# The weights of the post norm multiplied in ahead of the squares, in a float32 decoder trunk

## The chip, the cores and the metric

The kernel runs on one core of a Trainium2 chip. Its engines are named as in the profile: PE (TensorE, the matmuls), PEld (its weight loads), DVE (VectorE), ACT (ScalarE), POOL (GpSimd) and SP (SyncE, which issues DMAs here). The metric is the device time of one execution in microseconds (us), the median over runs.

## The reference, cut to what matters

Two layers, each of three stages: a feed-forward (SwiGLU, width 2816), a mixer (four branches, gated and summed, then an output projection), and a second feed-forward. Each stage is wrapped in two RMS norms, one ahead of it and one behind it (the post norm), and added to the residual stream h, which is 512 tokens x 1024 channels of float32.

```
def rms_norm(x, g):
    y = xf * lax.rsqrt(jnp.mean(xf * xf, axis=-1, keepdims=True) + EPS)
    return (y * g.astype(jnp.float32)).astype(x.dtype)
...
f = swiglu(rms_norm(h, ffn1_pre_g[l]), ffn1_w_gate[l], ffn1_w_up[l], ffn1_w_down[l])
h = h + FFN_RESIDUAL_SCALE * rms_norm(f, ffn1_post_g[l])
u = rms_norm(h, mix_pre_g[l])
...
h = h + rms_norm(merged @ w_o[l], mix_post_g[l])
f = swiglu(rms_norm(h, ffn2_pre_g[l]), ffn2_w_gate[l], ffn2_w_up[l], ffn2_w_down[l])
h = h + FFN_RESIDUAL_SCALE * rms_norm(f, ffn2_post_g[l])
```

The post norm needs, for each token, the sum of the squares of the projection's row (for the factor 1/sqrt) and the row itself times the weights g. The two don't depend on each other.

## The kernel before, in words

Every float32 matmul is done as three matmuls of rounded parts: a value is split into a high part (hi, written by ACT) and the rest (lo, written by DVE). Weights come in chunks of 128 x 1024 (`raw`, issued by SP or POOL); ACT casts a chunk to `wh` (L122, L109), DVE subtracts to get `wl` (L123, L110). There are five buffers for each of the two, so a cast waits until PE has done with an older chunk.

The function `boundary` (from L257) is the end of one stage and the start of the next; it is called seven times, the first time without an end, the last time without a start. The last projection of a stage (down projection or output projection) is done by tokens: four token tiles t of 128 tokens, two column halves c of 512. A tile and half is one PSUM bank, `py`, 128 x 512. The first half runs over k with four banks open at once, and `gained(t, 0, ...)` follows for the four tiles (L372). The second half is done so that the tiles end one after another: behind each tile come `gained(t, 1, ...)`, `update(t)` and `normed(t)` (L387 to L390), while PE works on the next tile.

In these:
- `gained` reads the bank twice: `squares` on ACT (L255, an activation `sq` that adds up its outputs in a column of `stat`, with a short read of the accumulator behind it) and a multiplication by the weights `gb` on DVE (L351), which writes `yg`.
- `update` makes the factor from the two sums of squares: `nv` (L249) and `nw` (L250) on DVE, a power `nr` on POOL (L251); then DVE adds to the residual, two instructions `h` (L356).
- `normed` takes the squares of the new `h` on ACT, stores `h` by DMA from ACT's queue (L274), makes the next factor in the same way and writes `u` on DVE (L278), the pre-normed tile.

`turned` transposes two token tiles of `u` on PE (L290, banks `pt`) and splits the result into `xh` (ACT, L175) and `xl` (DVE, L168), both of which read `pt`. `outer` starts the next stage's first four products in banks `pf`: for each of eight k and four f, matmuls L152 (`xh`, `wh`), L153 (`xl`, `wh`), L154 (`xh`, `wl`), first on the token half of tiles 0 and 1. When tile 3 has been updated too, its and tile 2's `u` are transposed and the second token half follows.

Within an engine instructions run in order. Around the change that order isn't written by hand: a scheduler places the instructions of all engines, by priority of program order and its own model of when operands are ready. From the start of the next stage's body on (`manual_schedule`) the side engines keep program order. Where two engines touch one bank, reads included, the framework makes the second in program order wait for the first by a semaphore.

Of the kernel before, what the change touches and what calls it, by code (L numbers as in the profile page):

```python
# [63 lines left out]
def build(tc, ws, x, vecs, gains, wdf, lamv, fb, consts, out):  # L64
# [3 lines left out]
    with ExitStack() as ctx:  # L68
# [12 lines left out]
        def nm(s):  # L81
            cnt[0] += 1
            return f"{s}{cnt[0]}"

        def slot(dt=F32, s="s"):
            return sp.tile([P, T], dt, tag="s", name=nm(s))

        def ps(s="p"):
            return pp.tile([P, T], F32, tag="p", name=nm(s))
# [10 lines left out]
        for l in range(DEPTH):  # L100
            for n in range(2):
                c = (2 * FFN_CHUNKS + MIX_CHUNKS) * l + (FFN_CHUNKS + MIX_CHUNKS) * n + PLAIN
# [10 lines left out]
        def load(c, parts=1):  # L113

            raw = rawp.tile([P, CB * P], F32, tag="raw", name=nm("raw"))
            wh = wp.tile([P, CB * P], F32R, tag="wh", name=nm("wh"))
            wl = wp.tile([P, CB * P], F32R, tag="wl", name=nm("wl"))
            n = CB * P // parts
            for i in range(parts):
                j = slice(i * n, (i + 1) * n)  # L120
                nc.sync.dma_start(out=raw[:, j], in_=ws[c, :, j])
                S.copy(out=wh[:, j], in_=raw[:, j])  # L122
                V.tensor_sub(out=wl[:, j], in0=raw[:, j], in1=wh[:, j].bitcast(F32))  # L123
            ready[c] = wh, wl
# [16 lines left out]
        def settle():  # L141
            while late:
                late.pop(0)()

        def cover():
            settle()
            for _ in range(min(pace[0], len(spare))):
                spare.pop(0)()
# [82 lines left out]
        def tile4(name, l, k, c):  # L231

            for j in range(4):
                block((name, l, k, c + P * j))
            b0 = (len(order) - 4) % CB * P
            return cur[0][:, b0:b0 + T], cur[1][:, b0:b0 + T]

        def by_tokens(out, x, t, w, first, last):

            r = slice(t * P, (t + 1) * P)  # L240
            PE.matmul(out=out, lhsT=x[0][:, r], rhs=w[0], start=first, stop=False)  # L241
            PE.matmul(out=out, lhsT=x[0][:, r], rhs=w[1], start=False, stop=False)  # L242
            PE.matmul(out=out, lhsT=x[1][:, r], rhs=w[0], start=False, stop=last)  # L243

        def rstd_of(parts, factor=1.0):

            f2 = factor * factor
            v, var, r = (np_.tile([P, 1], F32, tag=n, name=nm(n)) for n in ("nv", "nw", "nr"))
            V.tensor_scalar(out=v, in0=parts[0], scalar1=1.0 / (D * f2), scalar2=EPS / f2, op0=ALU.mult, op1=ALU.add)  # L249
            V.scalar_tensor_tensor(out=var, in0=parts[1], scalar=1.0 / (D * f2), in1=v, op0=ALU.mult, op1=ALU.add)  # L250
            G.tensor_tensor(out=r, in0=var, in1=mhalf[:, 0:1], op=ALU.pow)  # L251
            return r

        def squares(src, col):
            S.activation(out=slot(F32, "sq"), in_=src, func=AF.Square, accum_out=col)  # L255

        def boundary(post, pre, first):  # L257
# [9 lines left out]
            stat = np_.tile([P, 16], F32, tag="stat", name=nm("stat"))  # L267

            def normed(t):

                for c in range(2):
                    squares(hs[t][c], stat[:, 8 + 2 * t + c:9 + 2 * t + c])
                    if post is not None:
                        nc.scalar.dma_start(out=hd[t][c], in_=hs[t][c])  # L274
                r = rstd_of([stat[:, 8 + 2 * t + c:9 + 2 * t + c] for c in range(2)])
                us = [slot(F32, "u") for _ in range(2)]
                for c in range(2):
                    V.tensor_scalar(out=us[c], in0=hs[t][c], scalar1=r, scalar2=None, op0=ALU.mult)  # L278
                return us
# [41 lines left out]
            if post is None:  # L321
                for t in range(4):
                    for c in range(2):
                        hs[t][c] = slot(F32, "h")
                        nc.sync.dma_start(out=hs[t][c], in_=x[t * P:(t + 1) * P, c * T:(c + 1) * T])
                    load(t, 2 if t == 0 else 1)
                us = [normed(t) for t in range(4)]
            else:
                row, factor, name, l, ys = post
                n = len(ys)  # L330
                gb = []

                def fetch():
                    for c in range(2):
                        gb.append(slot(F32, "gb"))
                        nc.scalar.dma_start(out=gb[c], in_=gains[row:row + 1, c * T:(c + 1) * T].broadcast_to([P, T]))
                        for t in range(NQ):
                            hs[t][c] = slot(F32, "h")
                            nc.scalar.dma_start(out=hs[t][c], in_=hd[t][c] if row else
                                                x[t * P:(t + 1) * P, c * T:(c + 1) * T])  # L340

                def part(k):
                    if k < n and not isinstance(ys[k], tuple):
                        ys[k] = halves(ys[k])

                yg = [[None, None] for _ in range(4)]

                def gained(t, c, p):
                    squares(p, stat[:, 2 * t + c:2 * t + c + 1])
                    yg[t][c] = slot(F32, "yg")  # L350
                    V.tensor_mul(out=yg[t][c], in0=p, in1=gb[c])  # L351

                def update(t):
                    r = rstd_of([stat[:, 2 * t + c:2 * t + c + 1] for c in range(2)], factor)
                    for c in range(2):
                        V.scalar_tensor_tensor(out=hs[t][c], in0=yg[t][c], scalar=r, in1=hs[t][c],  # L356
                                               op0=ALU.mult, op1=ALU.add)
                        if pre is None:
                            (nc.sync, nc.scalar)[c].dma_start(out=out[t * P:(t + 1) * P, c * T:(c + 1) * T],
                                                              in_=hs[t][c])  # L360

                settle()
                py = [ps("py") for _ in range(4)]
                for k in range(n):
                    if k == n // 2:
                        fetch()
                    part(k + AHEAD)
                    w = tile4(name, l, k, 0)
                    for t in range(4):
                        by_tokens(py[t], ys[k], t, w, k == 0, k == n - 1)  # L370
                    cover()
                for t in range(4):  # L372
                    gained(t, 0, py[t])
                py = [ps("py") for _ in range(4)]
                for k in range(n - HOLD):
                    w = tile4(name, l, k, T)
                    for t in range(4):
                        by_tokens(py[t], ys[k], t, w, k == 0, False)
                held = []
                for t in range(4):  # L380
                    for k in range(n - HOLD, n):
                        if t == 0:
                            held.append(tile4(name, l, k, T))
                        if t == NQ - 1 and k == n - HOLD // 2 and pre is not None:
                            turned(us[0:2], 0)
                        by_tokens(py[t], ys[k], t, held[k - n + HOLD], k == 0, k == n - 1)
                    gained(t, 1, py[t])  # L387
                    update(t)
                    if pre is not None:
                        us.append(normed(t))  # L390
                if pre is None:
                    return None
# [77 lines left out]
        def halves(src):  # L470
            hi, lo = slot(F32R, "gh"), slot(F32R, "gl")
            hi_of(hi, src)
            lo_of(lo, src, hi)
            return hi, lo
# [536 lines left out]
        for l in range(DEPTH):  # L1011
            c = l * VL + _VOFF["b_conv_w"]
# [3 lines left out]
        for l in range(DEPTH):  # L1016
            post = ffn(l, 1, boundary(post, ("ffn1_pre_g", l), ffn_first(l, 1)))
            post = mixer(l, boundary(post, ("mix_pre_g", l), mix_first(l)))
            post = ffn(l, 2, boundary(post, ("ffn2_pre_g", l), ffn_first(l, 2)))
# [51 lines left out]
```

## Time and profile before

| | |
|---|---|
| median of 3 runs | 2692.07 us (2691.65 to 2693.31) |
| the profiled execution's own time | 2689.96 us |
| its span, first to last instruction | 2688.2 us |
| busy: PE, DVE, ACT, POOL | 98%, 61%, 44%, 9% |
| instructions | 39670 |
| mean granted TensorE clock | 0.999 |

The span is what the trace covers; the execution's own time is 1.8 us longer. Matmuls overlap in the array, so a PE that is busy isn't at its peak; its pace is read from the distance between starts. "Granted clock" is the share of full TensorE speed that the throttle allowed in a stretch. In a timeline a bracket at the end of a row gives the idle time ahead of it and what ended that.

### The profile page before, as it was taken

The numbers are of one execution on the slowest core, as the hardware profiler recorded it, in microseconds if no ns is written. First come the engines' busy times: TensorE is split into PE (matmuls) and PEld (weight loads), VectorE is DVE, ScalarE is ACT, GpSimd is POOL, SyncE is SP. The second block draws the span as 40 slices with busy tenths as digits, with TensorE's granted clock in tenths as the row PEclk, the third lists the DMA queues.
The fourth block names the chain that finished last, engine by engine and source line by source line (L and its number), as shares of the span: only waits on it lengthen the run. The fifth ranks groups of instructions, "written<-read, shape, count | busy, mean of one in ns | idle before, by whom it ended". The sixth has DMA issues, their size and how long they took to land.

```text
span 2688.2 us, 39670 instructions
## 1 busy us (share of the span) xinstructions
PE 2646.6 (98%) x15764; PEld 2352.2 (88%) x15764; DVE 1651.0 (61%) x2715; ACT 1195.6 (44%) x2031; POOL 234.7 (9%) x306
## 2 busy tenths in 40 slices
PE   6999999999999999999999999999999999999998
PEld 6999888888888889998899998888888888899987
DVE  5656358777776456555375563596786854565552
ACT  5445242355454335544255452424545533455541
POOL 2110000000000002110021100000000000111100
PEclk9999999999999999999999999999999999999999
DMA  6987433222223256885358872332223223488850
GB/s 182 214 212 202 134 113 102 87 79 79 91 83 94 95 163 153 210 205 187 102 139 210 210 217 94 121 101 79 71 87 96 86 92 96 150 186 211 201 171 32
DMA packets 110105, 365.26 MB, mean 136 GB/s; under 512 B 12496, under 2 KB 12880, under 8 KB 109920
## 3 DMA queue, kind: packets, MB, share of 16 engines
q1 hardware_dynamic: 68688, 246.45, 27.5%
q0 software_dynamic: 23040, 83.90, 17.8%
q10 hardware_dynamic: 18192, 32.40, 3.6%
q8 instruction: 123, 2.02, 0.3%
q14 instruction: 62, 0.51, 0.1%
HBM read 350.07 MB, written 12.62 MB: 135 GB/s over the span
## 4 chain that ended last, share of the span: by engine, by line
PE 83%; DVE 5%; issue 5%; DMA 4%; ACT 2%; POOL 1%; POOLq 0%; ACTq 0%; DVEq 0%
PE p L152 11%; PE p L154 10%; PE p L153 10%; PE f L154 7%; PE f L152 7%; PE f L153 7%; PE py L241 6%; PE py L243 6%; PE py L242 6%; DMA raw<-ws 4%; PE o L782 1%; PE pv L242 1%; PE pv L241 1%; PE pv L243 1%; PE pt L766 1%
## 5 line engine op out<-in xcount | busy, mean ns | idle before, releaser
L122 ACT CAST wh<-raw 128x1024 fp32r<-128x1024 f32 (+1 forms) x305 | 319.1, 1049 | 719.0 <-PE p L153 348.0
L123 DVE TENSOR_TENSOR wl<-raw,wh 128x1024 fp32r<-128x1024 f32 (+1 forms) x305 | 371.4, 1219 | 383.2 <-ACT wh L122 377.6
L110 DVE TENSOR_TENSOR wl<-raw,wh 128x1024 fp32r<-128x1024 f32 x280 | 335.5, 1222 | 196.7 <-ACT wh L109 196.0
L152 PE MATMUL p<-xh,wh 128*128 128x512 f32 x1024 | 404.1, 395 | 0.0
L154 PE MATMUL p<-xh,wl 128*128 128x512 f32 x1024 | 399.2, 390 | 0.0
L153 PE MATMUL p<-xl,wh 128*128 128x512 f32 x1024 | 398.7, 389 | 0.0
L152 PE MATMUL f<-th,wh 128*128 128x256 f32 x1280 | 363.4, 284 | 5.2 <-DVE f L513 2.5
L154 PE MATMUL f<-th,wl 128*128 128x256 f32 x1280 | 362.1, 284 | 2.9 <-DVE wl L110 2.9
L153 PE MATMUL f<-tl,wh 128*128 128x256 f32 x1280 | 362.4, 283 | 0.0
L109 ACT CAST wh<-raw 128x1024 fp32r<-128x1024 f32 x280 | 282.5, 1049 | 8.1 <-DMA raw<-ws 8.1
L241 PE MATMUL py<-wh,gh 128*128 128x512 f32 x704 | 274.2, 389 | 0.0
L242 PE MATMUL py<-wl,gh 128*128 128x512 f32 x704 | 273.9, 389 | 0.0
L243 PE MATMUL py<-wh,gl 128*128 128x512 f32 x704 | 273.9, 389 | 0.0
L152 PE MATMUL f<-xh,wh 128*128 128x256 f32 x960 | 271.7, 283 | 0.0
L153 PE MATMUL f<-xl,wh 128*128 128x256 f32 x960 | 271.3, 283 | 0.0
L154 PE MATMUL f<-xh,wl 128*128 128x256 f32 x960 | 269.9, 283 | 0.0
L152 PEld LDWEIGHTS f<-th,wh 128*128 128x128 f32 x1280 | 246.3, 192 | 6.7 <-DVE f L513 3.3
L154 PEld LDWEIGHTS f<-th,wl 128*128 128x128 f32 x1280 | 245.7, 192 | 4.3 <-DVE wl L110 4.3
L153 PEld LDWEIGHTS f<-tl,wh 128*128 128x128 f32 x1280 | 246.3, 192 | 0.0
L492 POOL DMA_DIRECT2D raw<-ws x160 | 140.0, 947 | 1065.9 <-DVE wl L110 577.0
L154 PEld LDWEIGHTS p<-xh,wl 128*128 128x128 f32 x1024 | 192.2, 188 | 40.8
L153 PEld LDWEIGHTS p<-xl,wh 128*128 128x128 f32 x1024 | 192.5, 188 | 39.1 <-issue 0.5
(211 smaller groups left out, 4792.5 us busy)
## 6 DMA issues: line engine op xcount, KB each, us to landing
raw<-ws SPq DMA_DIRECT2D x463, 512.0 KB, 3.7
raw<-ws POOLq DMA_DIRECT2D x160, 512.0 KB, 6.9
hd<-h ACTq DMA_DIRECT2D x40, 256.0 KB, 2.0
h<-hd ACTq DMA_DIRECT2D x40, 256.0 KB, 5.5
cb<-cum ACTq DMA_DIRECT2D x16, 256.0 KB, 3.6
gb<-gains ACTq DMA_DIRECT2D x12, 256.0 KB, 5.1
h<-x SPq DMA_DIRECT2D x8, 256.0 KB, 4.8
h<-x ACTq DMA_DIRECT2D x8, 256.0 KB, 5.4
```

The lines of the kernel that those rows point to most:

```text
L109: S.copy(out=wh, in_=raw)
L110: V.tensor_sub(out=wl, in0=raw, in1=wh.bitcast(F32))
L122: S.copy(out=wh[:, j], in_=raw[:, j])
L123: V.tensor_sub(out=wl[:, j], in0=raw[:, j], in1=wh[:, j].bitcast(F32))
L152: PE.matmul(out=out, lhsT=w[0], rhs=x[0], start=first, stop=False, skip_group_check=free)
L153: PE.matmul(out=out, lhsT=w[0], rhs=x[1], start=False, stop=False, skip_group_check=free)
L154: PE.matmul(out=out, lhsT=w[1], rhs=x[0], start=False, stop=last, skip_group_check=free)
L241: PE.matmul(out=out, lhsT=x[0][:, r], rhs=w[0], start=first, stop=False)
L242: PE.matmul(out=out, lhsT=x[0][:, r], rhs=w[1], start=False, stop=False)
L243: PE.matmul(out=out, lhsT=x[1][:, r], rhs=w[0], start=False, stop=last)
L492: G.dma_start(out=ga[g][key], in_=ws[base + 4 * g + u], accum_op=ALU.add)
L766: PE.transpose(out=p[:, (i - j) * P:(i - j + 1) * P], in_=rows[i][:, j * P:(j + 1) * P], identity=ident)
```

## The change

`gained` has its two readers of the bank in the other order: the multiplication by the weights is written first, the squares second. Nothing else is edited.

```
                 def gained(t, c, p):
-                    squares(p, stat[:, 2 * t + c:2 * t + c + 1])
                     yg[t][c] = slot(F32, "yg")
                     V.tensor_mul(out=yg[t][c], in0=p, in1=gb[c])
+                    squares(p, stat[:, 2 * t + c:2 * t + c + 1])
```

The multiplication is L350 afterwards in place of L351. The built programs hold the same instructions; POOL's and SP's orders are the same, DVE's, ACT's and PE's change at the stage ends. Three places, all at the end of the first feed-forward, ahead of the first mixer.

VectorE, tile 1 of the second half (a name's number is that of its buffer's allocation; in brackets stand the engines or queues whose semaphores the instruction waits for):

```order
 L278 TENSOR_SCALAR u_3687<-h_3182,nr_3682 128x512
-L351 TENSOR_TENSOR yg_3716<-py_3401,gb_3180 128x512 [waits Activation_49]
-L250 SCALAR_TENSOR_TENSOR nw_3719<-stat_2953,nv_3718 128x1 [waits DVE_49]
-L356 SCALAR_TENSOR_TENSOR h_3174<-yg_3390,nr_3720,h_3174 128x512 [waits Pool_49]
-L356 SCALAR_TENSOR_TENSOR h_3184<-yg_3716,nr_3720,h_3184 128x512 [waits DVE_49]
+L350 TENSOR_TENSOR yg_3714<-py_3401,gb_3180 128x512 [waits PE_49]
+L250 SCALAR_TENSOR_TENSOR nw_3719<-stat_2953,nv_3718 128x1 [waits Activation_49]
+L356 SCALAR_TENSOR_TENSOR h_3174<-yg_3388,nr_3720,h_3174 128x512 [waits Pool_49]
+L356 SCALAR_TENSOR_TENSOR h_3184<-yg_3714,nr_3720,h_3184 128x512 [waits DVE_49]
```

The order is the same; the multiplication waits for PE in place of ACT, and `nw` now waits for ACT. The squares of the same bank, on ScalarE, wait for PE before and for VectorE afterwards.

VectorE, behind the `u` of tile 2, where the first transposed tiles are split for the next stage (`wl` is the rest of a weight chunk, `xl` that of the transposed tile):

```order
 L278 TENSOR_SCALAR u_3791<-h_3186,nr_3786 128x512
+L123 TENSOR_TENSOR wl_3904<-raw_3902,wh_3903 128x1024 [waits DMAHW4_49,Activation_49]
 L168 SCALAR_TENSOR_TENSOR xl_3812<-pt_3806,vec,xh_3811 128x256 [waits Activation_49]
-L123 TENSOR_TENSOR wl_3904<-raw_3902,wh_3903 128x1024 [waits DMAHW4_49,Activation_49]
+L123 TENSOR_TENSOR wl_3934<-raw_3932,wh_3933 128x1024 [waits DMAHW5_49,Activation_49]
 L168 SCALAR_TENSOR_TENSOR xl_3816<-pt_3806,vec,xh_3815 128x256 [waits Activation_49]
-L123 TENSOR_TENSOR wl_3934<-raw_3932,wh_3933 128x1024 [waits DMAHW5_49,Activation_49]
 L168 SCALAR_TENSOR_TENSOR xl_3825<-pt_3819,vec,xh_3824 128x256 [waits Activation_49]
```

Two weight differences each move ahead of one `xl`; the first of them now stands ahead of the first `xl`. Their casts on ScalarE move in the same way, each ahead of one `xh`. At the ends that lead into a feed-forward the second of the two is one of L110.

PE, the start of the next stage's first products (`pf`):

```order
 L152 MATMUL pf_3898<-xh_3811,wh_3627 128x256
+L152 MATMUL pf_3899<-xh_3811,wh_3627 128x256
+L152 MATMUL pf_3900<-xh_3811,wh_3627 128x256
 L153 MATMUL pf_3898<-xl_3812,wh_3627 128x256
 L154 MATMUL pf_3898<-xh_3811,wl_3628 128x256
-L152 MATMUL pf_3899<-xh_3811,wh_3627 128x256
 L153 MATMUL pf_3899<-xl_3812,wh_3627 128x256
 L154 MATMUL pf_3899<-xh_3811,wl_3628 128x256
-L152 MATMUL pf_3900<-xh_3811,wh_3627 128x256
```

Two more matmuls that need only `xh` stand ahead of the first that needs `xl`. Further on, the twelve transposes of the second token half stand five `pf` matmuls earlier than before. The same three moves are at the other four stage ends that have a next stage.

## Rows read from the trace of the kernel before

**Rows 1.** Busy time of each engine, share of the span, instructions (page, part 1).

```profile
PE 2646.6 (98%) x15764; PEld 2352.2 (88%) x15764; DVE 1651.0 (61%) x2715; ACT 1195.6 (44%) x2031; POOL 234.7 (9%) x306
```

**Rows 2.** Waits of PE, whole span: us in total, times, longest us.

```profile
PE pt L290 <- DVE u L278: 17.7, 5, 14.3
PE pf L153 <- DVE xl L168: 7.1, 6, 2.0
```

**Rows 3.** Waits of DVE, whole span, same columns.

```profile
DVE yg L351 <- ACT sq L255: 45.6, 15, 9.3
```

**Rows 4.** Timeline of ACT, first stage end, tile 0: start us, us, what.

```profile
357.91 0.60 ACT L255 ACTIVATE sq<-py 128x512 f32<-128x512 f32 x1 [4.38 <-PE py L243]
358.40 0.19 ACT L255 ACTIVATION_READ_ACCUMULATOR sq<-py 128x1 f32 x1
```

**Rows 5.** Timeline of DVE, first stage end.

```profile
358.63 0.69 DVE L351 TENSOR_TENSOR yg<-py,gb 128x512 f32<-128x512 f32 x1 [3.85 <-ACT sq L255]
359.23 0.15 DVE L250 SCALAR_TENSOR_TENSOR nw<-stat,nv 128x1 f32<-128x1 f32 x1
...
363.22 0.88 DVE L278 TENSOR_SCALAR u<-h,nr 128x512 f32<-128x512 f32 x2 [0.73 <-POOL nr L251]
364.07 0.69 DVE L351 TENSOR_TENSOR yg<-py,gb 128x512 f32<-128x512 f32 x1
...
376.56 0.48 DVE L168 SCALAR_TENSOR_TENSOR xl<-pt,vec,xh 128x256 fp32r<-128x256 f32 x1
376.95 1.21 DVE L123 TENSOR_TENSOR wl<-raw,wh 128x1024 fp32r<-128x1024 f32 x1
378.09 0.47 DVE L168 SCALAR_TENSOR_TENSOR xl<-pt,vec,xh 128x256 fp32r<-128x256 f32 x1
...
383.52 0.48 DVE L168 SCALAR_TENSOR_TENSOR xl<-pt,vec,xh 128x256 fp32r<-128x256 f32 x1 [0.54 <-ACT xh L175]
384.09 0.69 DVE L351 TENSOR_TENSOR yg<-py,gb 128x512 f32<-128x512 f32 x1
```

**Rows 6.** Timeline of PE, start of the first mixer.

```profile
375.79 0.28 PE L152 MATMUL pf<-xh,wh 128*128 128x256 f32 x1
377.09 0.38 PE L153 MATMUL pf<-xl,wh 128*128 128x256 f32 x1 [1.02 <-DVE xl L168]
377.31 0.28 PE L154 MATMUL pf<-xh,wl 128*128 128x256 f32 x1
377.43 0.28 PE L152 MATMUL pf<-xh,wh 128*128 128x256 f32 x1
...
388.92 0.28 PE L152 MATMUL pf<-xh,wh 128*128 128x256 f32 x1
389.28 1.53 PE L290 MATMUL pt<-cst,u 128*128 128x128 f32 x12
```

**Rows 7.** Timeline of DVE, end of the first mixer, tile 1.

```profile
986.89 0.88 DVE L278 TENSOR_SCALAR u<-h,nr 128x512 f32<-128x512 f32 x2 [0.67 <-POOL nr L251]
987.85 0.69 DVE L351 TENSOR_TENSOR yg<-py,gb 128x512 f32<-128x512 f32 x1
```

**Rows 8.** Timeline of PE, start of the second feed-forward.

```profile
1012.71 0.28 PE L152 MATMUL pf<-xh,wh 128*128 128x256 f32 x1
1013.49 1.74 PE L290 MATMUL pt<-cst,u 128*128 128x128 f32 x12 [0.49 <-DVE u L278]
```

**Rows 9.** Stretches near the start: us, busy of PE, PEld, DVE, ACT, POOL, PE clock, DMA, GB/s.

```profile
53.50:56.00 2.50, 0.00 (x0) 0.00 (x0) 1.67 (x4) 1.82 (x5) 0.00 (x0) 0.93 0.94 175
56.00:58.95 2.95, 2.94 (x13) 2.94 (x14) 2.77 (x5) 1.98 (x3) 0.00 (x0) 0.50 0.76 149
```

**Rows 10.** Timeline of PE in the second of these stretches.

```profile
56.01 0.58 PE L152 MATMUL f<-th,wh 128*128 128x256 f32 x1 [2.54 <-DVE f L513]
...
56.60 0.41 PE L154 MATMUL f<-th,wl 128*128 128x256 f32 x1
56.82 0.41 PE L152 MATMUL f<-th,wh 128*128 128x256 f32 x1
```

More of the change, by code (lines that the diff above doesn't have):

```diff
@@ L348, in gained @@
                 def gained(t, c, p):
-                    squares(p, stat[:, 2 * t + c:2 * t + c + 1])
                     yg[t][c] = slot(F32, "yg")
                     V.tensor_mul(out=yg[t][c], in0=p, in1=gb[c])
+                    squares(p, stat[:, 2 * t + c:2 * t + c + 1])
                 def update(t):
```

## The prediction

> **What bounds the kernel now.** I read the busy table first: TensorE (PE) is busy for 98% of the span [rows 1], so the time is the matmuls plus the few moments in which PE has nothing to do. Then the waits of PE alone: apart from the start of the kernel (one wait of 14.3 us) the largest are two that return at every stage end, a matmul at L153 that waits for VectorE's xl, 1.0 us each, and a transpose at L290 that waits for VectorE's u [rows 2]. Both lie where the change is. Next the waits of VectorE: its multiplication yg waits for ScalarE's squares [rows 3]. Last the timeline of one stage end, the first feed-forward into the first mixer, engine by engine [rows 4 to 6], and of the next one, mixer into feed-forward, where it differs [rows 7, 8].
>
> What the reader is to see in them: at a stage end PE finishes one token tile after another. For each tile ScalarE squares the bank, VectorE multiplies it, then comes a serial chain nw, nr, h, squares of h, nw, nr, u. All of it hides behind the matmuls of the next tile until the third tile (t = 2): PE starts on the next stage at 375.79, has one L152 matmul to do, and then waits until the first xl is written, 377.09 [rows 6].
>
> **The change, part by part.** Nothing is added or removed: eight squares and eight multiplications at each of six stage ends, the same DMAs in the same queue order (POOL's and SP's orders are untouched). What turns round is who waits. The two read the same bank and are put one behind the other: today the multiplication starts 0.04 us after the squares end (358.40 + 0.19, then 358.63) [rows 4, 5]. Afterwards the squares wait for the multiplication, and nw waits for the squares.
>
> Tile 0. Today: squares at 357.91, nw at 359.23, 1.32 us [rows 4, 5]. Afterwards: multiplication 0.69, handover 0.04, squares with their accumulator read 0.68 (357.91 to 358.59), handover 0.04: 1.45 us. Cost 0.13. Two things are not shown: how soon VectorE starts after PE, and the handover from VectorE to ScalarE. The nearest row is the handover of 0.04 the other way; I take it, and 0.1 more or less for each tile as bounds.
>
> Tiles 1 and 2. Here VectorE is the late one: it is still writing u when PE is done, and ScalarE has squared meanwhile. The multiplication follows u directly (u at 363.22, yg at 364.07, 0.85 later) and nw comes 0.60 behind yg (358.63 to 359.23) [rows 5]. The squares were free; afterwards they stand behind the multiplication, on the chain: 1.45 in place of 0.60, so 0.85 for each tile. h of tile 2 is late by 0.13 + 0.85 + 0.85 = 1.83 us. Behind a mixer yg stands 0.96 behind u [rows 7], so 0.11 of slack goes first in each: 0.13 + 2 x 0.74 = 1.61.
>
> Then the order itself. The scheduler now puts one weight difference wl ahead of the first xl, on the engine PE is waiting for. Today it comes behind; start to start it takes 1.14 us (376.95 to 378.09) [rows 5]. Its cast on ScalarE moves ahead too, but VectorE is late enough for it to be done. First xl: 1.83 + 1.14 = 2.97 late (behind a mixer 2.75). PE has two more L152 matmuls to do ahead of it, 0.12 us each (377.31 to 377.43) [rows 6], so PE runs 2.97 - 0.24 = 2.73 (2.51) late, and its idle stretch grows from 1.02 to about 3.75 (3.5) us. For this price the bounds are 0, if the early wl fell into a gap of VectorE, and about 2.3, if VectorE also sits out that cast, a pass over as much data as the wl itself (1.21); I take 1.14, since the rows of VectorE stand without a gap there.
>
> Tile 3. The last xl is late by 1.83 only, since the wl that went ahead is no longer among the xl's. The multiplication no longer waits for squares: today it starts 0.57 behind the last xl (383.52 to 384.09), while an instruction that waits for nothing starts 0.39 behind an xl (376.56 to 376.95), so 0.18 is won [rows 5]. Then again 0.85. The last u, and with it the second set of transposes, is late by 1.83 - 0.18 + 0.85 = 2.50 (behind a mixer 2.28). PE now meets these transposes five matmuls earlier in its order, 5 x 0.12 = 0.60 us; it gets there 2.13 late (1.91) and waits again. The five are done behind them, so PE leaves the stage end 2.50 + 0.60 = 3.10 late (2.88). There are five such ends, three behind a feed-forward and two behind a mixer: 3 x 3.10 + 2 x 2.88 = 15.1 us. The sixth, at the end of the kernel, has no next stage: only tile 0's 0.13. Sum 15.2.
>
> The first halves (four multiplications and four squares behind the k loop) cost nothing: PE goes on with the second half in the other four banks, and the casts behind them are loaded three chunks ahead of their use (AHEAD). If that cover were gone, the casts on ScalarE would be late by about one multiplication, 0.69.
>
> **The clock.** In this trace PE idled 2.54 us ahead of 56.01, and when it came back the granted clock was 0.50, the lower of its two levels (1.2 of 2.4 GHz), until 58.95 [rows 9, 10]. Matmuls that start 0.12 us apart otherwise were 0.22 apart (56.60 to 56.82): 13 in 2.95 us where 13 x 0.12 = 1.56 would do, 1.39 lost; a restart at full clock loses 0.10 of that too (377.09 to 377.31) [rows 6], so 1.30. Idle stretches of 1.0 us at the stage ends left the clock alone: behind 377.31 matmuls start 0.12 apart [rows 6]. The new ones, 3.5 to 3.75 us, are longer than the one that lowered it, so I count 1.30 us at each of the five ends. Part of it falls into PE's second wait. Into a mixer PE has today 0.24 of wait there (388.92 + 0.12 to 389.28) [rows 6], afterwards 0.24 + 2.50 - 2.13 = 0.61, so 0.69 stays, twice. Into a feed-forward it is 0.66 today (1012.71 + 0.12 to 1013.49) [rows 8], afterwards 1.03, so 0.27 stays, three times. Sum 2.2 us. Bounds: 0, if the clock holds, and double the loss, 5 x 1.3 = 6.5 more.
>
> The Trainium skill ("TensorE: Matmul & The Clock Gate", Part 1, "What's actually happening") says that the throttled state is the default and that activity lifts it. By that rule the longer idle stretches fall back to 1.2 GHz each; the trace agrees where it has such a stretch (2.54 us, then 0.50).
>
> Total 15.2 + 2.2 = 17.4 us. The durations are of the profiled execution, 2689.96 us; it becomes 2707.3. It lies 2.1 us under the median of the runs, 2692.07, so the median becomes 2709.4; the times below go by the median.
>
> **Rivals.**
> A. The clock holds: 15.2 us alone, 2707.3. For it: the 1.0 us waits never lowered the clock. Against: 2.54 us did.
>
> B. The swap costs only its order: ScalarE and VectorE read the bank side by side, and the squares end where they did. Then nothing but the early wl and the transposes' place is left: PE 1.14 - 0.24 = 0.90 late at the first xl, of which the second wait takes some back and the transposes cost 0.60 less what they waited: about 0.6 an end, 3 us, 2695. Against: VectorE waits for the squares at 15 places, 45.6 us, today [rows 3], and in the new order the squares carry a wait for VectorE and nothing else.
> The Trainium skill ("PSUM — Partial Sum Buffer", "PSUM bank collisions raise a hardware error") says that two engines may not access one bank at once, two readers included, so that the wait must turn round with the order. By that rule B is out; the trace of before shows the one direction only.
>
> C. The other side: faster. Place: the end of each stage. If the squares still ended before nw is due, VectorE's multiplication would be rid of its wait, the transposes five matmuls earlier would find u written, and PE's two waits would go: 5 x 1.02 + 2 x 0.24 + 3 x 0.66 = 7.6 us, 2684.5. It decides from the point at which ScalarE finishes the squares before VectorE has finished the multiplication. Against: at tiles 1 to 3 the multiplication starts later than the squares do today, so squares behind it can't be earlier.
>
> D. More of the same: the clock takes twice as long to come back, or the shift of the casts makes a further wait in the feed-forward: 6.5 us more, 2716.
>
> **How the numbers follow.** Forecast (17.4 us, with the low clock at most of the ends) 0.58; A 0.22; B 0.09; C 0.04; D 0.07. The range is to hold 8 in 10: from 2702 (A with the early wl at the low side of its price) to 2714 (forecast with part of D). About 0.2%, 5.4 us, is what a measurement of this kernel can tell from no change: faster by more needs C, 0.04; within it B and a part of a very cheap A, 0.09; slower the rest, 0.87.
>
> **What would show it.** In the changed kernel's timeline at the first stage end: squares of a tile starting 0.03 behind the end of its multiplication; nw of tile 2 about 1.8 us later, measured from the end of PE's tile; one wl between u and the first xl; PE's wait at L153 up from 1.0 to about 3.5 to 3.75 us, five times; the granted clock at 0.50 just behind it; the transposes' wait 0.6 to 1.0 us, or gone where the clock fell. Waits elsewhere in the kernel should be as before. Wrong would be: waits at L153 that stay near 1 us (B), a clock that stays at full speed (A), or a loss in the middle of a stage, of which I have none in the sum.

## The result, and the profile after

The changed kernel takes 2708.93 us (median of 4 runs, 2707.48 to 2709.79) against 2691.86 us for the kernel before, timed beside it (4 runs, 2691.5 to 2693.31). The ratio is 1.0062, 95% interval 1.005 to 1.0075, so the change costs 17.1 us (13.5 to 20.2). Forecast were 17.4 us and 2709.4.

The profiled execution takes 2708.75 us, its span is 2707.0 us, its mean granted clock 0.995. The span is 18.8 us longer than that of before, but 2.7 of these lie ahead of the change: the transposes at the first stage end start at 374.00, before at 371.31. That start changes from execution to execution, whatever the edit: two runs below which leave most of the change out have it at 373.95 and 374.31, one with most of it in at 371.98. From there to the end the changed kernel is 16.1 us longer.

The busy table of the page answers to [rows 1]. The share of PE is the same 98% and its matmuls are as many, so no work was added. But PE is busy 7.9 us longer. From the first end's first transposes on it is 6.0 us (2296.41 and 2302.44), so of the 16.1 us some 6 are the same matmuls at a slower pace and some 10 are idle time.

```profile
PE 2654.5 (98%) x15764; PEld 2360.7 (87%) x15764; DVE 1653.8 (61%) x2715; ACT 1195.0 (44%) x2031; POOL 235.0 (9%) x306
```

The waits of PE (engine, line, whom it waited for: us in total, times, longest) answer to [rows 2].

```profile
PE pt L290 <- DVE u L278: 17.3, 2, 15.4
PE pf L153 <- DVE xl L168: 16.7, 6, 3.0
...
PE pf L152 <- ACT xh L175: 1.3, 5, 0.3
```

At L153 the total went from 7.1 to 16.7 us, that is from 1.0 to 3.0 at each of the five ends (the sixth, of 2.0 and 1.8 us, is at the start of the kernel). The transposes waited five times before and wait twice now; these two are at the start of the kernel in both, so at the stage ends the wait ahead of them is gone. A short new wait, 0.3 us, stands ahead of L152. Who waits for whom in the pair of readers has turned round: these are rows of ACT and of DVE, and answer to [rows 3].

```profile
ACT sq L255 <- DVE yg L350: 96.3, 30, 10.6
```

```profile
DVE yg L350 <- PE py L243: 29.4, 13, 8.6
DVE nw L250 <- ACT sq L255: 25.0, 39, 0.8
```

The timeline of ACT and of DVE at the first stage end (start us, us, what; in brackets the idle time ahead and what ended it) answers to [rows 4, 5].

```profile
361.32 0.60 ACT L255 ACTIVATE sq<-py 128x512 f32<-128x512 f32 x1 [5.11 <-DVE yg L350]
361.81 0.19 ACT L255 ACTIVATION_READ_ACCUMULATOR sq<-py 128x1 f32 x1
```

```profile
360.59 0.69 DVE L350 TENSOR_TENSOR yg<-py,gb 128x512 f32<-128x512 f32 x1 [3.13 <-PE py L243]
362.04 0.16 DVE L250 SCALAR_TENSOR_TENSOR nw<-stat,nv 128x1 f32<-128x1 f32 x1 [0.75 <-ACT sq L255]
...
366.04 0.88 DVE L278 TENSOR_SCALAR u<-h,nr 128x512 f32<-128x512 f32 x2 [0.73 <-POOL nr L251]
366.83 0.68 DVE L350 TENSOR_TENSOR yg<-py,gb 128x512 f32<-128x512 f32 x1
368.27 0.16 DVE L250 SCALAR_TENSOR_TENSOR nw<-stat,nv 128x1 f32<-128x1 f32 x1 [0.76 <-ACT sq L255]
...
380.12 0.88 DVE L278 TENSOR_SCALAR u<-h,nr 128x512 f32<-128x512 f32 x2 [0.73 <-POOL nr L251]
380.92 1.22 DVE L123 TENSOR_TENSOR wl<-raw,wh 128x1024 fp32r<-128x1024 f32 x1
382.06 0.48 DVE L168 SCALAR_TENSOR_TENSOR xl<-pt,vec,xh 128x256 fp32r<-128x256 f32 x1
```

The squares of tile 0 start at 361.32, 0.04 behind the end of the multiplication (360.59 + 0.69). From yg to nw it is 1.45 and 1.44 us. The multiplication of tile 1 starts 0.79 behind its u (366.04 to 366.83), where it was 0.85 before. Between u and the first xl stands one wl, which takes 1.14 from start to start.

PE at the start of the next stage, which answers to [rows 6]; first two lines of before, from which the shifts below are counted:

```profile
371.31 1.91 PE L290 MATMUL pt<-cst,u 128*128 128x128 f32 x16
...
390.56 0.36 PE L153 MATMUL pf<-xl,wh 128*128 128x256 f32 x1
```

```profile
374.00 1.91 PE L290 MATMUL pt<-cst,u 128*128 128x128 f32 x16
...
378.94 0.63 PE L152 MATMUL pf<-xh,wh 128*128 128x256 f32 x3 [0.30 <-ACT xh L175]
382.59 0.39 PE L153 MATMUL pf<-xl,wh 128*128 128x256 f32 x1 [3.02 <-DVE xl L168]
...
384.78 0.41 PE L154 MATMUL pf<-xh,wl 128*128 128x256 f32 x1
384.99 0.41 PE L153 MATMUL pf<-xl,wh 128*128 128x256 f32 x1
...
395.37 1.47 PE L290 MATMUL pt<-cst,u 128*128 128x128 f32 x12
396.60 0.36 PE L154 MATMUL pf<-xh,wl 128*128 128x256 f32 x1
```

PE idles 3.02 us, restarts at 382.59 at the full pace of 0.12 us, and from about 384.1 on its matmuls start 0.21 apart. The wait is shorter than the 3.5 to 3.75 us of the prediction, since its first L152 comes later: 4.94 us behind the end's first transposes (378.94 - 374.00), before 4.48 (375.79 - 371.31). It waits 0.30 there for ScalarE's xh, ahead of which a cast now stands, and three L152 take 0.63, one took 0.28. The twelve transposes at 395.37 wait for nothing. The stretches (us, busy of PE, PEld, DVE, ACT, POOL, granted clock, DMA share, GB/s) around this end, and around the second end further down, answer to [rows 9]:

```profile
378.94:382.55 3.61, 0.63 (x3) 0.41 (x3) 2.83 (x9) 0.88 (x1) 0.55 (x1) 1.00 0.80 279
382.59:384.10 1.51, 1.34 (x9) 1.13 (x9) 1.51 (x3) 0.82 (x2) 0.00 (x0) 0.97 0.64 144
384.10:387.60 3.50, 3.39 (x16) 3.42 (x17) 2.11 (x5) 1.95 (x5) 0.00 (x0) 0.52 0.74 240
387.60:392.90 5.30, 5.30 (x47) 5.30 (x46) 2.93 (x7) 2.23 (x7) 0.55 (x1) 1.00 0.13 46
```

```profile
1008.70:1009.14 0.44, 0.00 (x0) 0.00 (x1) 0.44 (x2) 0.02 (x1) 0.00 (x0) 0.50 0.44 177
1009.14:1011.80 2.66, 2.66 (x12) 2.66 (x13) 2.12 (x4) 1.58 (x4) 0.89 (x1) 0.50 0.66 205
```

The clock falls to 0.50, the lower level of 1.2 GHz, at all five ends: at the first, third and fifth 1.4 to 1.8 us after the restart, at the second and fourth 0.5 and 0.1 us ahead of it, so that a part of the slow stretch falls into the wait.

A table of the five ends, from the PE timelines of the two kernels. The first pair of lines is the shift of the L153 restart, measured from that end's own first set of transposes (371.31 and 374.00 at the first end); its forecast is that of the first xl, 2.97 or 2.75, from which the prediction then took 0.24 for two matmuls. The second pair is the shift of the first `pf` matmul behind the twelve transposes (390.56 and 396.60), with 0.12 us for each of the five matmuls that now stand behind them. The last line is the growth from one end's first transposes to the next end's (the last: to the end of the span).

| | end 1 | 2 | 3 | 4 | 5 | sum |
|---|---|---|---|---|---|---|
| L153 late, forecast | 2.97 | 2.75 | 2.97 | 2.97 | 2.75 | |
| L153 late, measured | 2.81 | 2.58 | 2.84 | 2.83 | 2.58 | |
| PE late behind the transposes, forecast | 3.79 | 3.15 | 3.37 | 3.79 | 3.15 | 17.3 |
| the same, measured | 3.95 | 2.74 | 3.38 | 3.47 | 3.15 | 16.7 |
| growth until the next end | 3.00 | 2.94 | 3.50 | 3.33 | 3.34 | 16.1 |

At the second end the transposes aren't free of waits: the twelve take 1.75 us there in place of 1.47, because those of the last tile wait for its u, done at 1022.13.

```profile
1021.31 1.75 PE L290 MATMUL pt<-cst,u 128*128 128x128 f32 x12
```

```profile
1020.30 1.83 DVE L278 TENSOR_SCALAR u<-h,nr 128x512 f32<-128x512 f32 x2 [0.73 <-POOL nr L251]
```

### The profile page after: what moved, and what is told of

It is laid out like the page before. It is cut to its first block, busy times and chain, and to the rows that moved or that the text cites. A ratio compares the mean times of both kernels' runs of the same rounds, so it can differ in the third digit from the quotient of the medians.

```text
span 2707.0 us, 39669 instructions
## 1 busy us (share of the span) xinstructions
PE 2654.5 (98%) x15764; PEld 2360.7 (87%) x15764; DVE 1653.8 (61%) x2715; ACT 1195.0 (44%) x2031; POOL 235.0 (9%) x306
## 4 chain that ended last, share of the span: by engine, by line
PE 87%; DVE 4%; DMA 3%; issue 2%; ACT 2%; POOL 1%; SPq 0%; DVEq 0%; ACTq 0%; POOLq 0%
PE p L152 11%; PE p L153 10%; PE p L154 10%; PE f L154 8%; PE f L152 8%; PE f L153 8%; PE py L243 6%; PE py L242 6%; PE py L241 6%; DMA raw<-ws 3%; PE pf L153 2%; PE pf L154 2%; PE pf L152 2%; PE o L782 1%; PE pv L241 1%
## 5 line engine op out<-in xcount | busy, mean ns | idle before, releaser
L110 DVE TENSOR_TENSOR wl<-raw,wh 128x1024 fp32r<-128x1024 f32 x280 | 335.7, 1223 | 197.1 <-ACT wh L109 196.5
L152 PE MATMUL p<-xh,wh 128*128 128x512 f32 x1024 | 404.2, 395 | 0.0
L153 PE MATMUL p<-xl,wh 128*128 128x512 f32 x1024 | 398.6, 389 | 0.0
L152 PE MATMUL f<-th,wh 128*128 128x256 f32 x1280 | 363.4, 284 | 5.5 <-ACT wh L109 2.7
L153 PE MATMUL f<-tl,wh 128*128 128x256 f32 x1280 | 362.5, 283 | 0.0
L152 PE MATMUL f<-xh,wh 128*128 128x256 f32 x960 | 271.7, 283 | 0.0
L153 PE MATMUL f<-xl,wh 128*128 128x256 f32 x960 | 271.3, 283 | 0.0
L152 PEld LDWEIGHTS f<-th,wh 128*128 128x128 f32 x1280 | 246.4, 192 | 7.0 <-DVE f L513 3.4
L153 PEld LDWEIGHTS f<-tl,wh 128*128 128x128 f32 x1280 | 246.4, 193 | 0.0
L153 PEld LDWEIGHTS p<-xl,wh 128*128 128x128 f32 x1024 | 192.5, 188 | 38.8 <-issue 0.5
```

The costliest lines, as they stand in the source:

```text
L110: V.tensor_sub(out=wl, in0=raw, in1=wh.bitcast(F32))
L152: PE.matmul(out=out, lhsT=w[0], rhs=x[0], start=first, stop=False, skip_group_check=free)
L153: PE.matmul(out=out, lhsT=w[0], rhs=x[1], start=False, stop=False, skip_group_check=free)
```

## The experiments

All comparisons are with the kernel before, timed beside the run: 2691.7 to 2692.4 us. My theory: the chain of the tiles (0.13 + 0.85 + 0.85), one wl ahead of the first xl, and the clock, the last in part covered by PE's second wait. Rivals: the early wl is free, or is nearly all; the clock's loss is all on the path, or none of it; the first halves cost something.

### The first halves alone

```
-                    squares(p, stat[:, 2 * t + c:2 * t + c + 1])
+                    first = c == 0
+                    if not first:
+                        squares(p, stat[:, 2 * t + c:2 * t + c + 1])
                     yg[t][c] = slot(F32, "yg")
                     V.tensor_mul(out=yg[t][c], in0=p, in1=gb[c])
+                    if first:
+                        squares(p, stat[:, 2 * t + c:2 * t + c + 1])
```

> Only the first halves (c = 0) have the multiplication ahead of the squares; the second halves are as before. My theory: 0 us (within 1 us of before), since PE goes on in the other four banks while ACT and DVE do these eight instructions; PE's two waits stay at 1.0 us (L153) and 0.2 to 0.7 us (transposes). Rival: the casts behind these squares come late, 0.69 us per stage end, about +4 us.

2692.15 us (11 runs) against 2691.73, ratio 1.0001 (0.9993 to 1.001). In its trace PE leaves the five ends within 0.01 us of before. The first halves are free.

### Tiles 1 and 2, and tile 3, of the second halves

The same edit with `first = c == 1 and t in (1, 2)`, and with `first = c == 1 and t == 3`.

> Only tiles 1 and 2 of the second halves have the multiplication ahead of the squares. VectorE's order is that of before but for these pairs (no early wl); two L152 more stand ahead of L153, the transposes stand where they did. My theory: 2 x 0.85 = 1.70 us later at h of tile 2 (1.48 behind a mixer), L153 1.46 (1.24) late, idle there 2.5 (2.3) us, long enough to lower the clock as in the run with the early wl held back; the last u is 1.70 (1.48) late. With 1.30 us for the clock and 0.24 or 0.66 of slack at the transposes PE leaves the ends 2.52, 1.88, 2.10, 2.52, 1.88 us late: +10.9 us. Rival: the clock costs nothing on the path and u sets the exit: 3 x 1.70 + 2 x 1.48 = +8.1 us. If only the chain up to h counted and tile 0 were the dear one, about +2.

> Only tile 3 of the second halves has the multiplication ahead of the squares; no early wl; the transposes of the second token half stand two matmuls later. My theory: L153 and its 1.02 us wait as before, clock at 1.0, last u later by 0.85 - 0.18 = 0.67 us, less 0.24 for the two matmuls now ahead of the transposes: 0.43 an end, +2.2 us (five ends). Rival: tiles 0 and 3 are alike, their squares wait and nothing behind them is late: 0 us.

Tiles 1 and 2: 2700.01 us (8 runs) against 2692.37, ratio 1.0027 (1.0016 to 1.0037), +7.6. L153 is 1.33 to 1.56 us late. In its trace the clock held at all five ends, and PE left them 1.57, 1.33, 1.57, 1.54 and 1.35 late, 0.13 to 0.16 less than the rival with the clock at no cost had it (1.70 and 1.48). So the chain costs about what was reckoned, and my expectation for the clock failed in this execution: waits of 2.1 to 2.35 us left it alone. The other executions of this run have no trace, but a mean clock: of the eight, four have 0.998 or 0.999, the traced one among them, and four 0.995 or 0.996. A slow stretch of 3.4 us takes 0.0006 off the mean, so by estimate the clock fell two or more times more in each of these four. They took 2700.6 us on average, the others 2699.3: the falls add little to the time here. The first line holds the wait, the second is the stretch up to the first four of the second set of transposes:

```profile
378.20:381.08 2.88, 0.53 (x5) 0.30 (x3) 2.10 (x8) 0.32 (x2) 0.55 (x1) 1.00 0.83 263
381.08:389.96 8.88, 8.60 (x69) 8.43 (x70) 6.43 (x12) 4.50 (x10) 0.55 (x1) 1.00 0.47 154
```

Tile 3: 2695.16 us (11 runs), ratio 1.0008 (0.9999 to 1.0017), +2.8. By time alone this can't be told from nothing; in the trace PE leaves the ends 0.42 to 0.44 us late, each of the five, where 0.43 was expected. That rests on one execution.

### The swap with the early wl held back

```
-            S.copy(out=wh, in_=raw)
-            V.tensor_sub(out=wl, in0=raw, in1=wh.bitcast(F32))
+            with ExitStack() as es:
+                for ins in queue.pop(0) if queue else ():
+                    es.enter_context(tc.issue_after(ins))
+                S.copy(out=wh, in_=raw)
+                V.tensor_sub(out=wl, in0=raw, in1=wh.bitcast(F32))
...
+                        if post is not None and h == 0 and k < 2:
+                            queue.append((a.ins if hasattr(a, "ins") else a, d.ins if hasattr(d, "ins") else d))
```

`a` and `d` are the instructions of an xh and an xl. `queue` holds the first two such pairs of a stage end; the casts and differences of the next two loaded chunks are placed behind them. The other place that casts a chunk has the same lines.

> The whole swap, but the weight casts and differences that had moved ahead of the first xh and xl are held behind them, as in the kernel before; DVE's order is then that of before but for the swapped pairs. My theory: the chain of three tiles alone, first xl 1.83 us late (1.61 behind a mixer), PE 0.24 less at L153, its idle there 2.4 to 2.6 us; the transposes stand 24 matmuls behind the start (22 before, 17 after), so PE leaves an end about 2.0 to 2.7 us late: +11 us against before, 6 less than the full change. Rival 1: the early wl fell into a gap of VectorE and cost nothing, then this equals the full change, +17 us. Rival 2: the order is most of it, then +3 us or less remain.

2702.38 us (5 runs) against 2691.73, ratio 1.0039 (1.0025 to 1.0052), +10.7 where 11 was expected; both rivals are out. The lines of this kernel are shifted: xl is L174, wl L130, `pf` L159 to L161, the transposes L295. VectorE has the first xl directly behind u, and L153 is 1.68 late at the first end, 1.13 less than with the early wl in front (1.14 reckoned):

```profile
380.17 0.88 DVE L283 TENSOR_SCALAR u<-h,nr 128x512 f32<-128x512 f32 x2 [0.73 <-POOL nr L256]
380.97 0.48 DVE L174 SCALAR_TENSOR_TENSOR xl<-pt,vec,xh 128x256 fp32r<-128x256 f32 x1
381.36 1.22 DVE L130 TENSOR_TENSOR wl<-raw,wh 128x1024 fp32r<-128x1024 f32 x1
```

So of the 17 us some 6 come from an instruction that has nothing to do with the swap and was moved by the scheduler (the transposes' place moved with it, 24 matmuls behind the start in place of 17).

### Tiles 0, 1 and 2

Here it is `first = c == 1 and t < 3`. Tile 0's swap, added to those of tiles 1 and 2, tips the scheduler: with it the wl stands ahead of the first xl, as it didn't with tiles 1 and 2 alone. The transposes stand 13 matmuls behind the first four of their set, not 17 as in the full change.

> Tiles 0, 1 and 2 of the second halves swapped, tile 3 as before. With tile 0 the scheduler puts the two wl ahead of the first xl again, as in the full change, and the transposes 17 matmuls behind the start. My theory: L153 as late as in the full change (2.6 to 2.8 us); the last u is 0.67 us earlier than there. If the clock falls at the ends, PE and not u sets the exit, and the time is that of the full change to within 1 us, +16. If it holds, +12 (L153 2.73 or 2.51 late less the slack at the transposes). Rival: the early wl isn't what separates the full change from the run that held it back; then about +8, as with tiles 1 and 2 alone.

2706.2 us (5 runs) against 2692.26, ratio 1.0057 (1.0043 to 1.0071), +13.9, lower than the +16 expected but with 16 inside the interval (11.6 to 19.1). L153 is 2.57 to 2.82 us late, as in the full change, and the clock fell at all five ends. PE leaves the ends 16.6 us late in sum, for 16.7 in the full change. That the sums agree is in part an accident: at the fourth end the slow stretch is twice as long as elsewhere, and PE leaves it 4.57 late; the other four come to 12.0, for 13.2 in the full change. So what tile 3 adds isn't settled by this run, neither by the sum nor by the time, which lies 3 us under that of the full change with an interval of 7.5. The rival (+8) is out.

### Sixteen extra matmuls in PE's wait

```
+                if post is not None and k == 0 and c == HALVES[0]:
+                    for _ in range(16):
+                        PE.matmul(out=pf[3][:, c], lhsT=blk[0][3][0], rhs=x[0], start=True, stop=True)
                 for f in range(4):
                     mm3(pf[f][:, c], blk[k][f], x, k == 0, k == KD - 1)
```

> The changed kernel, plus sixteen extra 128x256 matmuls at each of the five stage ends, written to a bank that is overwritten behind them, ahead of the first L152 (16 x 0.12 = 1.9 us of the 3.0 us that PE idles there). Their result isn't used. The transposes then stand 14 matmuls behind the start in place of 17. If the idle stretch lowers the clock, the granted clock stays at 1.0 at the ends and matmuls behind L153 start 0.12 us apart in place of 0.21. My theory for the time: PE then waits for u again, so at most 2.2 us are won, and about 0.36 us an end are lost to the transposes' place: 0 to -2 us against the changed kernel. Rival: the whole 1.30 us per end is on the path, -6.5 us. Second rival: the clock falls anyway, then 0.

> The changed kernel with sixteen extra matmuls at each end, a second execution under the profiler. In the first the clock fell at the second and fourth end and held at the others, with waits of 1.2 to 1.4 us at all of them. The same two ends again: it follows from the work around them. Other ends: it does not.

2708.35 us (5 runs), 1.0063 (1.005 to 1.0076): the time of the changed kernel, within the 0 to -2 us expected, which the time can't tell from the 0 of the second rival; the 6.5 us of the first rival aren't there. PE's wait at L153 is down to 1.2 to 1.4 us. The clock did not obey: it fell at the second and the fourth end in the first execution, at the third and the fifth in the second one. That gives the price of a fall directly, the same end with and without. The third end: in the first execution (clock held) the stretch from L153 to the first four of the second set of transposes, then these four in the second execution:

```profile
1364.26:1373.51 9.25, 8.85 (x72) 8.67 (x73) 6.12 (x12) 4.08 (x10) 1.45 (x2) 1.00 0.54 121
```

```profile
1374.81 0.60 PE L290 MATMUL pt<-cst,u 128*128 128x128 f32 x4
```

Without the fall 9.25 us, with it 10.74 (the second execution restarts at 1364.07): 1.49 us. Behind the twelve transposes only 0.48 of that is left (22.18 and 22.66 us from the end's first transposes), since in the first execution PE then waits 0.57 us for u.

### The changed kernel, and the one with the early wl held back, a second time

> The changed kernel again, a second execution under the profiler. If the granted clock at a stage end follows from the kernel's work, it falls at all five ends again, at the same places to within some tenths of a us. If it is a matter of chance or of the phase of what watches the engine, the number of ends or the places differ.

> The swap with the early wl held back, a second execution under the profiler. In the first the clock fell at all five ends with idle stretches of 2.2 to 2.5 us, while it held at all five with 2.1 to 2.35 us when only tiles 1 and 2 were swapped. Falls at all five again: it follows from the kernel. At fewer or other places: it does not follow from the length of the wait alone.

The changed kernel (2709.62 us): the clock fell at all five ends again, and PE left them 3.96, 2.75, 3.40, 3.31 and 3.18 us late, for 3.95, 2.74, 3.38, 3.47 and 3.15. The three executions without a trace have mean clocks of 0.994 and 0.995, as low as the two with one, so the five falls seem to belong to this kernel. With the early wl held back (2703.45 us) it fell at the last four ends and held at the first, where it had fallen before. These are the two executions at that end, the fall first:

```profile
381.50 0.39 PE L160 MATMUL pf<-xl,wh 128*128 128x256 f32 x1 [2.47 <-DVE xl L174]
391.88 0.60 PE L295 MATMUL pt<-cst,u 128*128 128x128 f32 x4
...
395.19 1.47 PE L295 MATMUL pt<-cst,u 128*128 128x128 f32 x12
```

```profile
381.35 0.39 PE L160 MATMUL pf<-xl,wh 128*128 128x256 f32 x1 [2.47 <-DVE xl L174]
390.23 0.60 PE L295 MATMUL pt<-cst,u 128*128 128x128 f32 x4
...
394.20 1.53 PE L295 MATMUL pt<-cst,u 128*128 128x128 f32 x12 [0.50 <-DVE u L283]
```

The same wait of 2.47 us, and then 10.38 or 8.88 us: 1.50 lost to the clock, of which 0.77 stays behind the second transposes (22.38 and 21.61 us), because in the other case PE waits 0.50 for u.

### The other way round: nw and the power ahead of the multiplication

If the position of the two readers counts, then the multiplication should go last: `h` needs it, but only after POOL's power.

```
                 def gained(t, c, p):
                     squares(p, stat[:, 2 * t + c:2 * t + c + 1])
+                    if c == 0:
+                        weighed(t, c, p)
+
+                def weighed(t, c, p):
                     yg[t][c] = slot(F32, "yg")
                     V.tensor_mul(out=yg[t][c], in0=p, in1=gb[c])
...
                     r = rstd_of([stat[:, 2 * t + c:2 * t + c + 1] for c in range(2)], factor)
+                    weighed(t, 1, py[t])
```

> The kernel before, squares first, with the second half's multiplication moved the other way: behind nw and the power, so that it runs while POOL computes nr. My theory: the multiplication, 0.60 us, leaves the chain of each tile, h of tile 2 comes 1.8 us earlier, PE's waits at L153 (1.0 us) and at the transposes (0.2 to 0.7 us) go: 5 x 1.02 + 2 x 0.24 + 3 x 0.66 = 7.6 us faster than before, about 2684.5. Rival: the power takes longer beside the multiplication or the chain waits for ACT's squares of h anyway; then 0 to -2 us.

2685.82 us (11 runs) against 2691.73, ratio 0.9978 (0.9969 to 0.9986): 5.9 us faster than before (3.8 to 8.3), a version that beats both kernels. The multiplication now lies in the 0.74 us for which VectorE used to wait for POOL:

```profile
366.99 0.16 DVE L250 SCALAR_TENSOR_TENSOR nw<-stat,nv 128x1 f32<-128x1 f32 x1 [0.56 <-ACT sq L255]
367.07 0.68 DVE L355 TENSOR_TENSOR yg<-py,gb 128x512 f32<-128x512 f32 x1
367.88 1.42 DVE L361 SCALAR_TENSOR_TENSOR h<-yg,nr,h 128x512 f32<-128x512 f32 x2
...
374.65 1.22 DVE L123 TENSOR_TENSOR wl<-raw,wh 128x1024 fp32r<-128x1024 f32 x1
375.79 0.21 DVE L249 TENSOR_SCALAR nv<-stat 128x1 f32<-128x1 f32 x2
375.91 1.22 DVE L123 TENSOR_TENSOR wl<-raw,wh 128x1024 fp32r<-128x1024 f32 x1
```

PE's wait at L153 is 0.27 us in place of 1.02, and PE leaves the ends 1.04 to 1.11 us earlier, 5.4 in sum; 7.6 needed all of the wait to go. The gain of 1.8 us at h of tile 2 was too much to ask: at tile 1 nw waits 0.56 us for the squares, which wait for PE, and two wl stand between tile 2's h and the nw ahead of its u (377.05).

## Why the prediction was right, point by point

**The first halves cost nothing.** Right, by the first run.

**The chain.** Right, and slightly too dear: 1.45 us from multiplication to nw at tile 0, 1.44 at tile 1, for 1.45 reckoned, but the multiplication follows u 0.06 sooner than before, so that tiles 1 and 2 cost 0.79 each and not 0.85. With them alone L153 is 1.33 to 1.56 late, for the 1.48 and 1.70 of the first xl; in the full change 2.58 to 2.84, for 2.75 and 2.97. The 0.24 us that two more L152 ahead of the wait were to give back were not gained: with the clock held, 69 matmuls from L153 to the next transposes take 8.88 us (tiles 1 and 2 alone), as 71 did before, since PE waits 0.28 us for the second xl. The two errors nearly cancel, and it is luck that 2.73 lies so near to 2.81. The handover from VectorE to ScalarE, which no row of before showed, is 0.04 us, as in the other direction.

**The early wl.** Right at 1.14 us, the value taken between bounds of 0 and 2.3: with it L153 is 2.81 late, without it 1.68.

**The two readers in turn (rival B).** Out: ACT's squares wait for DVE's multiplication 30 times, 96.3 us. The wait is a semaphore that the framework sets, so this shows the order and not what two readers at once would do. The Trainium skill ("PSUM — Partial Sum Buffer", "PSUM bank collisions raise a hardware error") says that two engines may not read one bank at once; no run here lets the two go at once, so the rule itself isn't shown.

**The clock.** That it falls at all five ends was right, in two executions. The size was off, and there is no single one: 1.46 to 1.51 us where the fall begins 1.5 us or more behind the restart, not 1.30, and less where it begins nearer to it. Against the 8.88 us of the same 69 matmuls with the clock held, a fall 0.8 us behind the restart costs 1.14 (third end, early wl held back: 10.02), and the one 0.5 us ahead of it, at the second end of the changed kernel, 0.76 (9.64). There a part of the slow stretch lies in the wait, and the 0.28 us for the second xl are not met; whether that is all of it isn't shown. The second and fourth end come out 0.41 and 0.32 us under the forecast. The step behind it, that an idle stretch longer than 2.54 us lowers the clock and one of 1.0 us doesn't, is only half a reason: waits of 2.1 to 2.35 us left it alone five times of five in the one trace of tiles 1 and 2 (and by the mean clocks not in four other executions), waits of 2.2 to 2.5 us went with a fall nine times of ten, and waits of 1.2 to 1.4 us behind sixteen matmuls four times of ten. What decides between these is open.

**What is covered.** I reckoned the exit from u (3.10 us late) plus what is left of the clock. The trace shows PE as the late one at four of the five ends: the transposes wait for nothing. From PE's side the sum is the same, 2.73 + 1.30 - 0.24 = 3.79, so the number stands, but there tile 3's term (-0.18 + 0.85, plus the five matmuls) isn't on the path. At the second end u sets the exit: its last part is 2.14 us later than before, for 2.28 reckoned, and with the five matmuls (0.60) that is the measured 2.74. At the others the last u is 2.15 to 2.35 later, for 2.28 and 2.50. Where the clock holds, as in the run with extra matmuls, PE waits for u again; so keeping the clock up won next to nothing.

**Waits elsewhere as before.** Not quite. The first mixer gives back 0.8 us of the 3.8 us by which PE comes to its attention part late. Before, ten transposes of its attention part wait twice for VectorE's e; afterwards PE comes when e is written. First before, then after:

```profile
705.94 0.45 PE L766 MATMUL pt<-cst,e 128*128 128x128 f32 x2
706.58 0.66 PE L766 MATMUL pt<-cst,e 128*128 128x128 f32 x4 [0.20 <-DVE e L939]
707.42 0.66 PE L766 MATMUL pt<-cst,e 128*128 128x128 f32 x4 [0.18 <-DVE e L939]
707.83 0.48 PE L152 MATMUL p<-xh,wh 128*128 128x512 f32 x1
```

```profile
712.42 1.32 PE L766 MATMUL pt<-cst,e 128*128 128x128 f32 x10
713.49 0.48 PE L152 MATMUL p<-xh,wh 128*128 128x512 f32 x1
```

1.89 us become 1.07. The parts add up: 16.7 us at the ends, less 0.8 in the first mixer, and 0.2 more elsewhere make the 16.1 us of the trace; the runs' medians say 17.1 (13.5 to 20.2).

**The total.** The mechanism was right, but that 17.4 meets 17.1 so closely is luck: the terms are off by 0.1 to 0.8 us in both directions, and by the trace alone the forecast is 1.3 us too high.

## What to carry to other kernels

Where two engines must read one buffer in turn, ask which result is needed first on the serial chain, and put the other reader where that chain waits for a third engine anyway: one order cost 17 us, the other won 6. When an edit makes a step longer in a scheduler's eyes, look what else it moves onto the engine that is waited for; a third of the loss here was a weight pass that the edit doesn't mention. Before counting a slower stretch (a clock, a burst) in full, look for the next wait of the same engine, which takes a part of it back.

## What the runs showed of the hardware

The granted clock didn't follow from the length of the idle stretch ahead of it: the same program, with the same 1.36 us wait at its third end, was granted 1.00 behind it in one execution and 0.50 in the next. It also fell late, some 1.5 us after PE had restarted at full pace (382.59, then 0.50 from about 384.1 on); at other ends it fell up to 0.5 us ahead of the restart or as much as 2.2 us behind it. Most of these slow stretches ran about 3.4 us; one, at the fourth end of the run with tiles 0 to 2, twice as long, 5.8 us of it behind the restart, and that end was the latest of its five (PE 4.57 us late, the others 2.60 to 3.44). Over the 27 falls of the usual length in the traces, the later a fall came behind the restart the more it cost up to the next transposes: 0.76 us at 0.5 us ahead of it, 1.14 at 0.8 us behind it, and about 1.5 from 1.5 us on.
